# Turning the tiles of v: VectorE blocks of 32x32 and transfers of 128-byte rows in place of TensorE

## The chip, the cores and the metric

The kernel runs on one core of a Trainium2 chip. The metric is the device time of one execution in microseconds (us). Before the change it is 1673.76 us, the median of three runs (1672.92 to 1674.23).

## What is computed

A backbone of two layers over 256 latent tokens and 256 context tokens of width 1024. Layer 0 mixes tokens with a convolution module, layer 1 with a bidirectional mLSTM of four heads; an MLP follows each. The change lies in layer 1, in the features of the mLSTM:

```python
up = u @ w_up
xm, z = up[..., :MLSTM_INNER], up[..., MLSTM_INNER:]      # MLSTM_INNER = 2048
xc = jax.nn.silu(dwconv(xm, w_conv) + b_conv)
q, k, v = xc @ w_q, xc @ w_k, xm @ w_v
gates = jnp.concatenate([q, k, v], axis=-1) @ w_gate + b_gate
...
num = jnp.einsum('bhts,bhsd->bhtd', scores, vc) + ...     # v with tokens as the contraction
```

All data is float32. The scan needs v with the tokens on the partitions; the product xm @ w_v is made with the features on the partitions, so each tile of v has to be turned.

## The kernel before

Each weight tile is loaded by SyncE's queue (`raw_load`, L143, 1 MB into one of three buffers `raw`), cut into two halves of 128x1024, and each half is split into a high part `wh` (a cast on ScalarE, L149) and a low part `wl` (a subtraction on VectorE, L150). Four buffers of each exist. A half then feeds 24 matmuls (L180, L183, L184: high by high, high by low, low by high, for eight blocks of the contraction). A scheduler of the framework sets the order of each engine's instructions; the program's order is its priority. Every transfer is given one of eight completion semaphores in turn (DMAHW0 to DMAHW7), over all queues, and waits until the transfer that had the semaphore before it has landed.

The stage that matters here makes v: `gemm_steps(wv, range(8), xm, T, v_epi)`. It yields sixteen tiles, m = 0 to 15, of 128 features by 512 tokens (four blocks of 128 tokens). `v_epi` (L1220) copies a tile out of PSUM to `vt` on ScalarE. Turning it is deferred: `v_out(m, vt)` is put in the list `late`, and `flush()` empties the list when the next even m is done, so two tiles are turned at a time. `v_out` first adds the tile's share of the gates for every fourth m (L1211, four matmuls), then turns the tile and writes it to a DRAM buffer `v_dr[head]` of shape 128 tokens x 4 blocks x 512 features, from which the attention part loads it later. The turned tile passes through one of the four buffers of the tag E.

Beside this stage the same loop loads `wqT` (two loads of 1 MB per two halves in its first part), multiplies it by the gate weights (L772, sixteen small matmuls at a time), and in its second part streams `ada_w` through VectorE (L417 loads, L421 and L425) and prepares the tiles `u` and `xc` of the queries (`xc_load`, L149 and L150 on 128x256). After it come the queries (L195, L196), whose weights `wq` go through `raw`, `wh` and `wl` as well.

Of the kernel before, what the change touches and what calls it, by code (L numbers as in the profile page):

```python
# [14 lines left out]
P = 128  # L15
# [55 lines left out]
def hybrid_kernel(ctx: ExitStack, tc: tile.TileContext, xT, vecs_d, wdw_d, ada0_w, ada_w, wg_d, pw1a, pw1, pw2, w1_0, w2_0,  # L71
                  w1_1, w2_1, up_x, up_z, wv, wo, bo_d, wk, wq, wqT, wdown, rows_d, out):
    nc = tc.nc
# [10 lines left out]
    def nm(s):  # L84
        uid[0] += 1
        return f"{s}_{uid[0]}"
# [3 lines left out]
    def tmp(tag, dt=F32):  # L90
        return tp.tile([P, T], dt, tag=tag, name=nm(tag), bufs={"E": 4, "S": 2, "L": 2, "F": 1}[tag])
# [8 lines left out]
    def psum(tag="mm"):  # L100
        return pp.tile([P, 512], F32, tag=tag, name=nm(tag), bufs={"mm": 3, "ln": 2, "fl": 1, "cv": 2}[tag])
# [23 lines left out]
    ident = con.tile([P, P], F32, name="ident")  # L125
# [1024 lines left out]
    v_dr = [dp.tile([P, 4, DH], F32, name=f"v_dr{h}") for h in range(H)]  # L1150
# [18 lines left out]
    for f in range(0, DT, 2):  # L1169
        t, tr = tmp("S"), psum("cv")  # L1170
# [39 lines left out]
    def gate_acc(j, w, t, last=False):  # L1210
        nc.tensor.matmul(gps[32 * j:32 * j + 32, :], w, t, start=j not in seen, stop=last,  # L1211
                         tile_position=(0, 32 * j), skip_group_check=True)
        seen.add(j)
# [4 lines left out]
    def v_epi(m, ps):  # L1218
        vt = B("vt").rearrange("p a b -> p (a b)")[:, :T]
        nc.scalar.copy(vt, ps)  # L1220
        vts.append(vt)
        if m % 2 == 0:
            flush()
        late.append(lambda: v_out(m, vt))

    def v_out(m, vt):
        if m % 4 == 3:
            for j in range(4):
                gate_acc(j, wgv[:, m - 3 + j, :], vts[m - 3 + j])
        tr = psum("ln")  # L1230
        for b in range(4):
            nc.tensor.transpose(tr[:, b * P:(b + 1) * P], vt[:, b * P:(b + 1) * P], ident)
        vk = tmp("E")
        nc.scalar.copy(vk, tr)
        nc.scalar.dma_start(v_dr[m // 4][:, :, (m % 4) * P:(m % 4 + 1) * P], vk.rearrange("p (b c) -> p b c", b=4))

    late = []

# [752 lines left out]
```

## Time and profile before

| | |
|---|---|
| median of 3 runs | 1673.76 us (1672.92 to 1674.23) |
| the profiled execution | 1674.57 us, span 1672.9 us, mean TensorE clock 0.998 |
| TensorE (PE) busy | 1660.0 us |
| VectorE (DVE), ScalarE (ACT) busy | 1034.3 and 744.0 us |
| DMA | 301.63 MB, 180 GB/s over the span |
| turns of v on TensorE (L1232) | 64 of 128x128, first at 765.0, last at 927.1 us |
| copies of the turned tiles (L1234) | 16 on ScalarE, 594 ns each |
| transfers to v_dr (L1235) | 16 of 256 KB, issued by ScalarE's queue |

How to read it: a line names the source line, the engine, the operation, the output and inputs, and the shape; behind the bar stand busy time, the mean duration of one, and the idle time before it with what ended it. Timeline rows have the start in us from the span's start and the duration. PEld is TensorE's weight load, which overlaps the matmuls; ACTq and SPq are the DMA issues of ScalarE and SyncE; q1 is SyncE's DMA queue and q10 ScalarE's, with packets, MB and the share of 16 engines that the packets took.

### The profile page before, as it was taken

How to read it: one execution, taken by the hardware profiler on the slowest of the kernel's cores; microseconds unless marked ns; L12 is line 12 of the kernel's file. 1: busy time of each engine (PE TensorE's matmuls, PEld its weight loads, DVE VectorE, ACT ScalarE, POOL GpSimd, SP SyncE). 2: the span in 40 equal slices, each digit the busy share in tenths (PEclk: the TensorE clock that was granted, in tenths of full speed). 3: DMA queues.
4: the chain of work that ended last, by engine and by line, in shares of the span. 5: the costliest groups of instructions: out<-in, count | busy, mean ns of one | idle time of the engine just before them, and what ended most of it. 6: DMA issues, size and time to landing. Idle time of an engine off the chain costs nothing. (4 is left out here: it accounts for less than half of the span.)

```text
span 1672.9 us, 22919 instructions
## 1 busy us (share of the span) xinstructions
PE 1660.0 (99%) x8928; PEld 1366.8 (82%) x8928; DVE 1034.3 (62%) x1877; ACT 744.0 (44%) x1196; POOL 14.3 (1%) x64
## 2 busy tenths in 40 slices
PE   9999999999999999999999999999999999999998
PEld 6665898888888998877788899888878888778887
DVE  6555895666635776752143653564389876786677
ACT  4313573232324476652232532442368654555453
POOL 0000000000000000000000000000000000000001
PEclk9999999999999999999999999999999999999999
DMA  9565213444424065556685753455375555675452
GB/s 356 202 215 207 88 71 114 151 135 139 142 101 151 1 210 187 183 195 248 254 271 168 262 175 120 136 205 170 133 246 192 193 210 211 249 272 190 182 186 92
DMA packets 73902, 301.63 MB, mean 180 GB/s; under 512 B 7519, under 2 KB 23683, under 8 KB 43969
## 3 DMA queue, kind: packets, MB, share of 16 engines
q1 hardware_dynamic: 56080, 285.44, 48.5%
q10 hardware_dynamic: 17712, 14.72, 2.6%
q8 instruction: 70, 1.15, 0.3%
q14 instruction: 40, 0.32, 0.1%
HBM read 284.37 MB, written 15.77 MB: 179 GB/s over the span
## 5 line engine op out<-in xcount | busy, mean ns | idle before, releaser
L150 DVE TENSOR_TENSOR wl<-raw,wh 128x1024 fp32r<-128x1024 f32 x344 | 418.7, 1221 | 275.7 <-ACT wh L149 273.2
L149 ACT CAST wh<-raw 128x1024 fp32r<-128x1024 f32 x344 | 359.3, 1052 | 509.6 <-PE mm L183 277.2
L183 PE MATMUL mm<-u,wh 128*128 128x512 f32 (+1 forms) x808 | 291.7, 361 | 0.2 <-DVE u L610 0.2
L180 PE MATMUL mm<-u,wh 128*128 128x512 f32 (+1 forms) x680 | 244.4, 360 | 0.1
L184 PE MATMUL mm<-u,wl 128*128 128x512 f32 (+1 forms) x680 | 241.4, 356 | 0.0
L183 PEld LDWEIGHTS mm<-u,wh 128*128 128x128 f32 x808 | 152.6, 189 | 23.1 <-issue 1.0
L180 PEld LDWEIGHTS mm<-u,wh 128*128 128x128 f32 x680 | 128.5, 189 | 25.7 <-issue 6.4
L184 PEld LDWEIGHTS mm<-u,wl 128*128 128x128 f32 x680 | 128.4, 189 | 18.8 <-issue 1.0
L211 PE MATMUL mm<-wh,xl 128*128 128x512 f32 x256 | 101.1, 395 | 0.0
L180 PE MATMUL mm<-xm,wh 128*128 128x512 f32 x256 | 101.0, 395 | 0.0
L212 PE MATMUL mm<-wh,xl 128*128 128x512 f32 x256 | 100.1, 391 | 0.0
L184 PE MATMUL mm<-xm,wl 128*128 128x512 f32 x256 | 99.7, 390 | 0.0
L213 PE MATMUL mm<-wl,xl 128*128 128x512 f32 x256 | 99.2, 391 | 0.1
L180 PE MATMUL mm<-hid,wh 128*128 128x512 f32 (+1 forms) x256 | 93.3, 364 | 0.0
L183 PE MATMUL mm<-hid,wh 128*128 128x512 f32 (+1 forms) x256 | 92.9, 363 | 0.0
L184 PE MATMUL mm<-hid,wl 128*128 128x512 f32 (+1 forms) x256 | 92.8, 363 | 0.0
L195 PE MATMUL mm<-x,wh 128*128 128x512 f32 x232 | 81.1, 398 | 0.0
L425 DVE SCALAR_TENSOR_TENSOR S<-ar,cs,S 128x512 f32<-128x512 f32 x56 | 40.8, 749 | 59.0 <-DMA ar<-ada_w 58.9
L183 PE MATMUL mm<-qq,wh 128*128 128x272 f32 x256 | 73.9, 289 | 0.0
L180 PE MATMUL mm<-qq,wh 128*128 128x272 f32 x256 | 73.5, 288 | 0.0
L184 PE MATMUL mm<-qq,wl 128*128 128x272 f32 x256 | 73.5, 288 | 0.0
L195 PE MATMUL mm<-u,wh 128*128 128x512 f32 x192 | 68.7, 399 | 0.0
(535 smaller groups left out, 3265.5 us busy)
## 6 DMA issues: line engine op xcount, KB each, us to landing
raw<-w SPq DMA_DIRECT2D x64, 1024.0 KB, 4.8
raw<-wo SPq DMA_DIRECT2D x32, 1024.0 KB, 4.8
raw<-ada_w SPq DMA_DIRECT2D x22, 1024.0 KB, 6.7
ar<-ada_w SPq DMA_DIRECT2D x80, 256.0 KB, 3.7
raw<-wv SPq DMA_DIRECT2D x16, 1024.0 KB, 7.1
raw<-wqT SPq DMA_DIRECT2D x16, 1024.0 KB, 6.2
raw<-wq SPq DMA_DIRECT2D x16, 1024.0 KB, 4.9
raw<-wk SPq DMA_DIRECT2D x16, 1024.0 KB, 4.9
```

The source lines that it names most:

```text
L149: c = nc.scalar.copy(hi, src)
L150: lastsub[0] = nc.vector.tensor_tensor(lo, src, hi.bitcast(F32), op=ALU.subtract).ins
L180: a = nc.tensor.matmul(ps, wh, xh, start=start, stop=False)
L183: nc.tensor.matmul(ps, wh, xl, start=False, stop=False)
L184: lastmm[0] = nc.tensor.matmul(ps, wl, xh, start=False, stop=stop).ins
L195: todo = [lambda s_, e_: nc.tensor.matmul(ps, wh, r[0], start=s_, stop=e_), lambda s_, e_: nc.tensor.matmul(ps[:, :n], wl, r[0][:, :n], st ...
L211: nc.tensor.matmul(ps, xh, wh, start=start, stop=False)
L212: nc.tensor.matmul(ps, xl, wh, start=False, stop=False)
L213: nc.tensor.matmul(ps, xh, wl, start=False, stop=stop)
L425: nc.vector.scalar_tensor_tensor(a, w, c, a, op0=ALU.mult, op1=ALU.add)
```

## The change

For every tile the four turns on TensorE and the copy out of PSUM are replaced by one VectorE instruction that turns the tile in blocks of 32x32 in place. What the blocks leave undone, bringing each block to its place, is left to the transfer: one of 128x4 rows of 512 bytes becomes four, one for each 32 partitions, and each writes 32x16 rows of 128 bytes (64 KB).

```diff
         if m % 4 == 3:
             for j in range(4):
                 gate_acc(j, wgv[:, m - 3 + j, :], vts[m - 3 + j])
-        tr = psum("ln")
-        for b in range(4):
-            nc.tensor.transpose(tr[:, b * P:(b + 1) * P], vt[:, b * P:(b + 1) * P], ident)
         vk = tmp("E")
-        nc.scalar.copy(vk, tr)
-        nc.scalar.dma_start(v_dr[m // 4][:, :, (m % 4) * P:(m % 4 + 1) * P], vk.rearrange("p (b c) -> p b c", b=4))
+        nc.vector.transpose(vk, vt)
+        for q in range(4):
+            f0 = (m % 4) * P + 32 * q
+            nc.scalar.dma_start(v_dr[m // 4][:, :, f0:f0 + 32].rearrange("(q i) b j -> i b q j", i=32),
+                                vk[32 * q:32 * q + 32, :].rearrange("i (b q j) -> i b q j", b=4, q=4))
```

The scheduler places the instructions anew. First, TensorE before, where tiles 0 and 1 are turned: mm_6870 is the sum of tile m=2, mm_6871 of m=3, mm_7032 of m=4, and wh_7002 and wh_7036 are the high parts of two weight halves.

```order
L184 MATMUL mm_6870<-xm_6713,wl_6945 128x512
L1232 MATMUL ln_6974<-ident,vt_6825 128x128 x4
L1232 MATMUL ln_6982<-ident,vt_6868 128x128 x4
L772 MATMUL fl_6827<-raw_6990,wgq_578 32x512 x4
L772 MATMUL fl_6827<-raw_6996,wgq_578 32x512 x4
L180 MATMUL mm_6871<-xm_6358,wh_7002 128x512
...
L184 MATMUL mm_6871<-xm_6713,wl_7003 128x512
L180 MATMUL mm_7032<-xm_5950,wh_7036 128x512
```

After the change the two rows of L1232 are gone from here and nothing else moves; the half behind L772 uses weights that were split earlier, and the one after that uses wh_7036 (wh_7032 in the changed kernel). ScalarE before, at the cast of those weights, with the semaphores that each row waits for:

```order
L149 CAST wh_7036<-raw_7034 128x1024 [waits DMAHW7_49,PE_49]
L1220 COPY vt_6972<-mm_6870 128x512 [waits PE_49]
L1234 COPY E_6979<-ln_6974 128x512 [waits DMAHW2_49,PE_49]
L1234 COPY E_6987<-ln_6982 128x512 [waits PE_49]
L1235 DMA v_dr_5286<-E_6979 512x1x128 [waits Activation_49]
L1235 DMA v_dr_5286<-E_6987 512x1x128 [waits Activation_49]
L149 CAST wh_7076<-raw_7034 128x1024
```

And after, at the same place, where E_6974 and E_6980 are the turned tiles 0 and 1 and DVE_49 is VectorE's semaphore:

```order
L1234 DMA v_dr_5286<-E_6974 128x4x32 [waits DVE_49]
L1234 DMA v_dr_5286<-E_6974 128x4x32 x2
L1234 DMA v_dr_5286<-E_6974 128x4x32 [waits DMAHW3_49]
L1234 DMA v_dr_5286<-E_6980 128x4x32 [waits DMAHW4_49,DVE_49]
L1234 DMA v_dr_5286<-E_6980 128x4x32 [waits DMAHW5_49]
L1234 DMA v_dr_5286<-E_6980 128x4x32 [waits DMAHW6_49]
L1220 COPY vt_6972<-mm_6870 128x512 [waits PE_49]
L1234 DMA v_dr_5286<-E_6980 128x4x32 [waits DMAHW0_49]
L149 CAST wh_7032<-raw_7030 128x1024 [waits DMAHW2_49]
L149 CAST wh_7072<-raw_7030 128x1024
```

Eight issues now stand ahead of the cast, and five of them wait for an earlier transfer (DMAHW6 and DMAHW0 there are the first two transfers of tile 0). At the end of the stage, ScalarE before, around the copy of tile 15 (vt_8037); wh_8181 and wh_8209 are the wq weights of the second half of the contraction:

```order
L149 CAST wh_8181<-raw_8179 128x1024 [waits DMAHW6_49,DVE_49]
L149 CAST u_8096<-raw_8076 128x256 [waits PE_49]
L149 CAST u_8097<-raw_8076 128x256 [waits PE_49]
L149 CAST wh_8209<-raw_8179 128x1024 [waits DVE_49,PE_49]
L1220 COPY vt_8037<-mm_7893 128x512 [waits PE_49]
L1234 COPY E_8047<-ln_8042 128x512 [waits PE_49]
L1235 DMA v_dr_5289<-E_8047 512x1x128 [waits DMAHW2_49,Activation_49]
```

After, from the copy of tile 15 (vt_8009) on; between the last two rows stand eight casts of xc; wh_8149 holds the same weights as wh_8181 before:

```order
L1220 COPY vt_8009<-mm_7869 128x512 [waits PE_49]
L1234 DMA v_dr_5289<-E_8014 128x4x32 [waits DMAHW6_49]
L1234 DMA v_dr_5289<-E_8024 128x4x32 [waits DMAHW0_49,DVE_49]
L1234 DMA v_dr_5289<-E_8024 128x4x32 [waits DMAHW1_49]
L1234 DMA v_dr_5289<-E_8024 128x4x32 [waits DMAHW2_49]
L1234 DMA v_dr_5289<-E_8024 128x4x32 [waits DMAHW3_49]
L149 CAST u_8059<-raw_8044 128x256
L149 CAST u_8064<-raw_8044 128x256
L149 CAST u_8065<-raw_8044 128x256
...
L149 CAST wh_8149<-raw_8147 128x1024
```

The cast of these weights has moved from ahead of tile 15 to behind its transfers and the casts of u and xc.

## The prediction

> **What bounds the kernel now.** I read the page first: engines, then the chain that ended last.
>
> ```profile
> span 1672.9 us, 22919 instructions
> PE 1660.0 (99%) x8928; PEld 1366.8 (82%) x8928; DVE 1034.3 (62%) x1877; ACT 744.0 (44%) x1196; POOL 14.3 (1%) x64
> PE 12%; DVE 0%; DVEq 0%; issue 0%
> ```
>
> TensorE is busy for 1660.0 of 1672.9 us and the chain that could be followed is TensorE alone. So TensorE work that goes away shortens the run, unless something else then comes late. The stage to look at is the one that makes v, about 740 to 930 us; the busy table of that stretch and its groups by shape:
>
> ```profile
> core 0: us, PE busy (x) PEld busy (x) DVE busy (x) ACT busy (x) POOL busy (x), PEclk, DMA share, GB/s
> 800.00:850.00 50.00, 50.00 (x255) 36.69 (x254) 14.51 (x21) 16.14 (x26) 0.00 (x0) 1.00 0.74 270
> sum 195.00, PE 195.00 PEld 147.30 DVE 66.52 ACT 64.00 POOL 0.00; mean PE 39.00 PEld 29.46 DVE 13.30 ACT 12.80 POOL 0.00
> ```
>
> ```profile
> L150 DVE TENSOR_TENSOR wl<-raw,wh 128x1024 fp32r<-128x1024 f32 x32 | 38.6, 1221 | 68.4 <-ACT wh L149 68.3
> L425 DVE SCALAR_TENSOR_TENSOR S<-ar,cs,S 128x512 f32<-128x512 f32 x14 | 10.5, 751 | 36.0 <-DMA ar<-ada_w 36.0
> L1232 PE MATMUL ln<-ident,vt 128*128 128x128 f32 x64 | 9.2, 276 | 0.0
> L1234 ACT COPY E<-ln 128x512 f32<-128x512 f32 x16 | 8.9, 594 | 1.6 <-PE ln L1232 1.6
> L421 DVE TENSOR_SCALAR S<-ar,cs 128x512 f32<-128x512 f32 x2 | 1.0, 482 | 2.9 <-DMA ar<-ada_w 2.9
> ```
>
> TensorE is full at full clock, VectorE and ScalarE work a third of the time, and the DMA engines are the next thing that is nearly used up (0.74 of the stretch from 800).
>
> **What goes away.** 64 turns on TensorE and 16 copies on ScalarE. The 276 ns of a turn is a pipelined duration; what it holds TensorE for is read from starts (TensorE's timeline):
>
> ```profile
> 764.76 0.39 PE L184 MATMUL mm<-xm,wl 128*128 128x512 f32 x1
> 764.99 1.03 PE L1232 MATMUL ln<-ident,vt 128*128 128x128 f32 x8
> 765.95 1.92 PE L772 MATMUL fl<-raw,wgq 128*32 128x512 f32 x16
> 767.81 0.50 PE L180 MATMUL mm<-xm,wh 128*128 128x512 f32 x1
> 773.17 0.39 PE L184 MATMUL mm<-xm,wl 128*128 128x512 f32 x1
> 773.40 0.39 PE L180 MATMUL mm<-xm,wh 128*128 128x512 f32 x1
> 778.61 0.39 PE L184 MATMUL mm<-xm,wl 128*128 128x512 f32 x1
> 778.93 1.92 PE L772 MATMUL fl<-raw,wgq 128*32 128x512 f32 x16
> ```
>
> From L184 to L772 it takes 1.19 us with eight turns between (764.76 to 765.95) and 0.32 without (778.61 to 778.93): eight turns cost 0.87 us, 0.11 each, and 64 cost 7.0 us. That is the whole possible gain, 0.42% of the run. It is the first term: -7.0.
>
> **What is added, off the path.** Sixteen block turns on VectorE. No row shows one; a pass over 128x512 takes 482 ns (L421) to 751 ns (L425), and an added instruction gains nothing; 0.6 us, 10 us in all, against 66.5 us of VectorE work in 195. Each waits for its vt, and VectorE's splits wl stand behind it. The buffer it writes is one of four, so it also waits for the transfers of four tiles earlier, some 40 us back.
>
> The transfers: 16 of 128x4 rows of 512 bytes become 64 of 512 rows of 128 bytes. The issues on ScalarE's queue (two source lines), and queue counts in three stretches (768 to 780, 560 to 620, 760 to 935):
>
> ```profile
> L1235 ACTq DMA_DIRECT2D v_dr<-E x16: 520/521/1534, 768.8 to 928.0; - x16
> DMA to landing us min/median/max: 2.4/4.1/10.5
> ```
>
> ```profile
> q10 hardware_dynamic: 1056, 0.52, 14.6%
> ```
>
> ```profile
> q10 hardware_dynamic: 1440, 1.31, 6.3%
> ```
>
> ```profile
> q1 hardware_dynamic: 6883, 36.60, 59.6%
> q10 hardware_dynamic: 8525, 4.29, 8.2%
> ```
>
> An issue takes 0.521 us; the new ones make 512 rows as well, so I take the same, up to 0.8 back to back (1.534 was the longest). ScalarE then spends 4 x 0.521 = 2.08 us a tile instead of 0.594 + 0.521 = 1.12: 15 us more in 195, room enough, if nothing urgent stands behind. Time on the DMA engines: 14.6% of 12 us x 16 engines is 28.0 us for 1056 packets, 26.5 ns at a mean of 496 bytes; 6.3% of 60 x 16 is 60.5 us for 1440, 42.0 ns at 910. The line through both gives 12.7 ns at 128 bytes (my estimate); the bounds are 12.7 and 26.5, and I take the low end because both rows lie on a slope with length. 32,768 rows are 2048 an engine: 26 us (54 at 26.5 ns) instead of 13.6. Loads use 104 us of the 175 per engine (59.6%), so the engines stay below full either way. A flush of two tiles holds them 256 x 12.7 ns = 3.3 us instead of 1.7, so a load that runs beside it lands up to 1.6 us later, within the cover of 4 us shown below.
>
> [...]
>
> **What comes late instead.** Each transfer carries one of eight semaphores in turn and waits until the last transfer on it has landed; ScalarE waits in order, and the casts of the weights wh stand behind. Two places matter.
>
> First, the flush of tiles 0 and 1, whose transfers stand ahead of the cast of the next weights. ScalarE's timeline there:
>
> ```profile
> 757.04 0.34 ACTq L1204 DMA_DIRECT2D zs_dr<-E  x1
> 766.75 1.05 ACT L149 CAST wh<-raw 128x1024 fp32r<-128x1024 f32 x1 [9.75 <-DMA raw<-wv]
> ```
>
> By the order, the cast at 766.75 serves the half that starts at 773.40. With the turns gone that half starts at 772.5 and wants wl 0.45 us in, so the cast may start until 770.6. Ahead of it now the last transfer of tile 1 waits for the second of tile 0, issued about 757.9 (behind zs_dr at 757.04, 0.34, and one issue of 0.52). It must land by 770.0: 12 us, where 10.5 was the longest. So nothing is lost if the rows keep to that; 1 us for every us beyond. The later flushes have the same cover of 4 to 5 us. For all of them I put 0.9 us, between 0 and 4.
>
> Second, the end of the stage. Tile 15 is ready when m=15 ends, and ScalarE has then five issues, three u casts and eight xc casts ahead of the cast of the wq weights which TensorE wants next; before, these weights were cast ahead of tile 15. Rows of TensorE, then of ScalarE:
>
> ```profile
> 923.54 0.39 PE L184 MATMUL mm<-xm,wl 128*128 128x512 f32 x1
> 923.77 0.60 PE L1232 MATMUL ln<-ident,vt 128*128 128x128 f32 x4
> 932.52 0.39 PE L195 MATMUL mm<-u,wh 128*128 128x512 f32 x1
> 932.75 0.28 PE L196 MATMUL mm<-u,wl 128*128 128x256 f32 x1
> ```
>
> ```profile
> 919.99 0.75 ACT L149 CAST u<-raw 128x256 fp32r<-128x256 f32 x2 [0.79 <-ACT E L1234]
> 924.69 0.58 ACT L1220 COPY vt<-mm 128x512 f32<-128x512 f32 x1
> 928.57 2.26 ACT L149 CAST xc<-raw 128x256 fp32r<-128x256 f32 x7 [0.28 <-ACT xc L149]
> ```
>
> Count from 923.77, the end of m=15 on TensorE. It wanted the weights of the second contraction half at 932.52, 8.75 us on; without its two groups of four turns (0.9) that is 7.85, and wl 0.23 later, 8.1. ScalarE: vt from 0.16 (its last matmul ends 923.93) to 0.75; last issue of tile 14 to 1.27; block turn of tile 15 to about 1.4; four issues to 3.5; three u casts at 0.375 to 4.6; eight xc casts at 0.32 to 7.2; cast 1.05 to 8.25; wl on VectorE 1.22 to 9.5. TensorE waits 9.5 - 8.1 = 1.4 us; with issues at 0.8 us, 2.8. I take 2.1.
>
> **The sum.** -7.0 + 2.1 + 0.9 = -4.0 us. The profiled execution took 1674.57 us (span 1672.9 and 1.67 around it, untouched): 1670.57. It lies 0.81 above the median of 1673.76, so the prediction is **1669.8 us**.
>
> **The rivals.**
> - All hidden: no wait takes the turns' place, for instance because TensorE's order reaches wl later. For it: VectorE and ScalarE are idle two thirds of the stage. Against: the end of the stage above. 1673.76 - 7.0 = 1666.8.
> - The gain is eaten: issues near 1 us each, or waits of 4 us in the flushes, as a stage that lives on loads (0.74 busy) gives back what TensorE saves. -7.0 + 2.8 + 3 = -1.2: 1672.6.
> - Slower through ScalarE's queue: the 128-byte rows share the engines with 1 MB loads, so a transfer lands after 15 us instead of 12 and each of eight flushes holds the next cast 3 us too long: -7 + 24, 1691. It decides from a landing of about 13 us on. For it: 10.5 has been seen with a quarter of the transfers. Against: the new transfers carry 64 KB instead of 256.
> [...]
> - The change doesn't do what it says: excluded, the built order has 64 fewer turns.
>
> **How the numbers follow.** Forecast 0.34, all hidden 0.10, eaten 0.16, ScalarE's queue 0.24, short rows 0.16. The two slower cases together get 0.40 because the price of a short row, on which both hang, is an extrapolation beyond the last row shown. Within 0.2% (3.3 us, about what a measurement of this kernel can tell from no change) is the eaten case alone: faster 0.44, same 0.16, slower 0.40. The forecast's own range is 1667 to 1670.4. The range that holds 8 in 10 starts at 1666.8, takes in the ScalarE case to 1692 and leaves out the short rows (0.16).
>
> **What would show it.** Right: no L1232 on TensorE; about 0.32 us from L184 to L772 at each flush; one wait of 1.5 to 3 us on wh or wl at the first query matmuls; v_dr issues near 0.52 us. Wrong: a q10 share in the stage above 25%, L149 behind L1234 with waits on v_dr transfers, repeated TensorE waits between 765 and 920, or block turns over 1.2 us.

## The result, and the profile after

The changed kernel took 1683.78 us (1682.70 to 1687.12) against 1673.99 before: ratio 1.0059, interval 1.0048 to 1.0071. It is slower by 9.8 us, where 4 us less were forecast. The parts of the page that answer to those of before (the head, the engines, the chain that ended last):

```profile
span 1681.1 us, 22846 instructions
PE 1658.7 (99%) x8864; PEld 1362.5 (81%) x8864; DVE 1044.1 (62%) x1893; ACT 733.0 (44%) x1180; POOL 14.3 (1%) x64
PE 89%; DMA 5%; DVE 4%; ACT 1%; issue 1%; DVEq 0%; ACTq 0%; SPq 0%
```

The 64 turns are gone from TensorE (8864 instructions for 8928), but the chain, which could be followed only along TensorE before, now leads through DMA and VectorE. The waits of TensorE between 740 and 1000 us, in total, times and longest (before there is no such row):

```profile
PE mm L184 <- DVE wl L150: 4.5, 1, 4.5
PE mm L195 <- DVE E L206: 2.9, 2, 1.8
PE mm L196 <- DVE wl L150: 1.3, 1, 1.3
PE mm L195 <- ACT wh L149: 1.2, 2, 0.6
```

Where the time went is read from the starts of the same matmuls. First TensorE's timeline, two rows of L180 on either side of the long wait, before and after the change:

```profile
890.21 0.39 PE L180 MATMUL mm<-xm,wh 128*128 128x512 f32 x1
903.15 0.39 PE L180 MATMUL mm<-xm,wh 128*128 128x512 f32 x1
```

```profile
885.79 0.39 PE L180 MATMUL mm<-xm,wh 128*128 128x512 f32 x1
905.45 0.39 PE L180 MATMUL mm<-xm,wh 128*128 128x512 f32 x1
```

Then the query matmuls of L195 in the view of their line (durations, first and last start), before and after:

```profile
L195 PE MATMUL mm<-u,wh x192: 387/397/502, 925.3 to 1109.1; 128*128 128x512 f32 x192
```

```profile
L195 PE MATMUL mm<-u,wh x192: 387/396/505, 926.2 to 1116.4; 128*128 128x512 f32 x192
```

At the first row of L180 the change had brought 4.42 us (890.21 to 885.79), as the forty turns up to there promised. At the second, sixteen L180 later, it was 2.30 us behind (903.15 to 905.45): 6.7 us were lost in between. That is net: the eight turns of tiles 10 and 11, which lie in this stretch before the change, are 0.9 us of gain, so 7.6 us were lost. The queries began 0.9 us late and ended 7.3 us late: 6.4 us more. The last 0.9 us up to the end of the span (8.2) come later; TensorE waits there for 1.7 us at L1402, and this was not followed.

**The first loss** is one wait and the slow clock behind it. The timeline of the changed kernel, rows of VectorE, then of ScalarE, then one of TensorE (start, duration, operation, and in brackets the idle time before it):

```profile
880.49 0.75 DVE L425 SCALAR_TENSOR_TENSOR S<-ar,cs,S 128x512 f32<-128x512 f32 x1 [3.84 <-DMA ar<-ada_w]
881.16 0.70 DVE L1231 STREAM_TRANSPOSE E<-vt 128x512 f32<-128x512 f32 x1
885.71 0.75 DVE L425 SCALAR_TENSOR_TENSOR S<-ar,cs,S 128x512 f32<-128x512 f32 x1 [3.85 <-DMA ar<-ada_w]
889.65 0.75 DVE L425 SCALAR_TENSOR_TENSOR S<-ar,cs,S 128x512 f32<-128x512 f32 x1 [3.19 <-DMA ar<-ada_w]
893.57 0.75 DVE L425 SCALAR_TENSOR_TENSOR S<-ar,cs,S 128x512 f32<-128x512 f32 x1 [3.17 <-DMA ar<-ada_w]
894.24 3.49 DVE L150 TENSOR_TENSOR wl<-raw,wh 128x1024 fp32r<-128x1024 f32 x3
877.26 0.82 ACTq L1234 DMA_DIRECT2D v_dr<-E  x1
881.89 0.58 ACTq L1234 DMA_DIRECT2D v_dr<-E  x1
885.68 2.95 ACT L149 CAST wh<-raw 128x1024 fp32r<-128x1024 f32 x3 [7.86 <-DMA v_dr<-E]
895.51 0.80 PE L184 MATMUL mm<-xm,wl 128*128 128x512 f32 x1 [4.50 <-DVE wl L150]
```

TensorE's busy time and granted clock there (the table of stretches; the clock is the column behind POOL):

```profile
890.00:895.00 5.00, 1.02 (x6) 0.30 (x2) 1.83 (x3) 0.84 (x2) 0.00 (x0) 0.96 0.18 52
895.00:900.00 5.00, 4.49 (x11) 3.52 (x12) 4.85 (x6) 0.00 (x0) 0.00 (x0) 0.50 0.80 271
900.00:905.00 5.00, 5.00 (x21) 4.06 (x20) 1.14 (x2) 0.59 (x1) 0.00 (x0) 0.85 0.92 262
```

Read it in order of time. VectorE's sum of ada_w at 880.49 waited 3.84 us for its load. The turn of tile 11 stood behind it, at 881.16. ScalarE's next transfer, the first of that tile, could go only when the turn was done, at 881.89; ScalarE's queue had been free since 878.08 (877.26 and 0.82). The cast of the next weights stood behind the four transfers of the tile, until 885.68; the third of these also waited 1.2 us, and by the numbers in the kernel's order the semaphore that it waited for (DMAHW0) had last been used by a transfer of tile 10, not by a load. The split wl of these weights then stood on VectorE behind three more sums of ada_w, whose loads come one at a time, some 4 us apart. It began at 894.24, and TensorE, which wanted it at 891.01, went on at 895.51. The rows of VectorE's order say the same; before, at most two sums stood between two splits:

```
L1231 STREAM_TRANSPOSE E_7826<-vt_7686 128x512
L425 SCALAR_TENSOR_TENSOR S_7723<-ar_7832,cs,S_7723 128x512
L425 SCALAR_TENSOR_TENSOR S_7723<-ar_7865,cs,S_7723 128x512
L425 SCALAR_TENSOR_TENSOR S_7723<-ar_7900,cs,S_7723 128x512
L150 TENSOR_TENSOR wl_7836<-raw_7784,wh_7835 128x1024
```

After the wait the clock was granted at 0.50 and then 0.85. In stretches of 1 us it is 1.00 up to 894, 0.82 from 894 to 895, still in the wait, 0.50 from 895 to 901, 0.77 from 901 to 902 and 1.00 from there. So TensorE, at work again from 895.51, ran some 6 us at 0.50 (up to about 901.5), its matmuls 0.43 us apart (twelve from 896.11 to 901.23) and 0.23 afterwards, and by that lost 3.0 us (an estimate, half of the 6). With the 4.50 us of the wait that makes 7.5 of the 7.6.

**The second loss** begins at the third load of wq. SyncE's timeline of the changed kernel, then a row of ScalarE and one of VectorE:

```profile
917.15 0.33 SPq L143 DMA_DIRECT2D raw<-wq  x1
928.16 0.33 SPq L1274 DMA_DIRECT2D rk<-wg_d  x1
930.95 0.33 SPq L143 DMA_DIRECT2D raw<-wq  x1
929.39 1.02 ACT L149 CAST u<-raw 128x256 fp32r<-128x256 f32 x3 [3.44 <-DMA v_dr<-E]
929.83 1.10 DVE L150 TENSOR_TENSOR u<-raw,u 128x256 fp32r<-128x256 f32 x3 [3.13 <-ACT u L149]
```

And before, the row of SyncE with two loads of wq (at 914.30 and, 9.97 us being the time to the end of the second, near 924), and the last split of u on VectorE:

```profile
914.30 9.97 SPq L143 DMA_DIRECT2D raw<-wq  x2
923.50 0.42 DVE L150 TENSOR_TENSOR u<-raw,u 128x256 fp32r<-128x256 f32 x1 [0.20 <-ACT u L149]
```

There are three buffers `raw`. The third load of wq takes the one from which the tiles u are split, so it must wait for the last of these splits. In both kernels it goes 0.02 us after that split has ended: at 923.94 before (923.92) and at 930.95 after (930.93). The last three splits come late because their casts stand on ScalarE behind the transfers of tile 15, which wait for the turn of that tile. The small load rk now stands ahead of this load of wq, but it has gone at 928.16, well before the buffer comes free. The loads of wq stay late through the queries, where TensorE waits five times.

### The profile page after: what moved, and what is told of

Same layout as the page of the kernel before. It is cut to its first block, busy times and chain, and to the rows that moved or that the text cites. A ratio compares the mean times of both kernels' runs of the same rounds, so it can differ in the third digit from the quotient of the medians.

```text
span 1681.1 us, 22846 instructions
## 1 busy us (share of the span) xinstructions
PE 1658.7 (99%) x8864; PEld 1362.5 (81%) x8864; DVE 1044.1 (62%) x1893; ACT 733.0 (44%) x1180; POOL 14.3 (1%) x64
## 4 chain that ended last, share of the span: by engine, by line
PE 89%; DMA 5%; DVE 4%; ACT 1%; issue 1%; DVEq 0%; ACTq 0%; SPq 0%
PE mm L180 16%; PE mm L184 16%; PE mm L183 16%; PE mm L195 5%; DMA ar<-ada_w 4%; PE mm L211 4%; PE mm L213 4%; PE mm L212 4%; PE mm L196 3%; PE cv L211 2%; PE cv L212 2%; PE cv L213 2%; PE fl L342 1%; PE ln L180 1%; DVE wl L150 1%; PE cv L855 1%
## 5 line engine op out<-in xcount | busy, mean ns | idle before, releaser
L180 PE MATMUL mm<-u,wh 128*128 128x512 f32 (+1 forms) x680 | 244.4, 360 | 0.0
L184 PE MATMUL mm<-u,wl 128*128 128x512 f32 (+1 forms) x680 | 241.5, 356 | 0.0
L180 PEld LDWEIGHTS mm<-u,wh 128*128 128x128 f32 x680 | 128.5, 189 | 25.6 <-issue 5.9
L184 PEld LDWEIGHTS mm<-u,wl 128*128 128x128 f32 x680 | 128.4, 189 | 18.9 <-issue 1.0
L184 PE MATMUL mm<-xm,wl 128*128 128x512 f32 x256 | 101.2, 395 | 4.5 <-DVE wl L150 4.5
L180 PE MATMUL mm<-xm,wh 128*128 128x512 f32 x256 | 102.0, 398 | 0.0
L180 PE MATMUL mm<-hid,wh 128*128 128x512 f32 (+1 forms) x256 | 93.3, 364 | 0.0
L184 PE MATMUL mm<-hid,wl 128*128 128x512 f32 (+1 forms) x256 | 92.8, 363 | 0.0
L195 PE MATMUL mm<-x,wh 128*128 128x512 f32 x232 | 81.1, 398 | 0.0
L180 PE MATMUL mm<-qq,wh 128*128 128x272 f32 x256 | 73.5, 289 | 0.0
L184 PE MATMUL mm<-qq,wl 128*128 128x272 f32 x256 | 73.5, 288 | 0.0
L195 PE MATMUL mm<-u,wh 128*128 128x512 f32 x192 | 69.3, 400 | 4.1 <-DVE E L206 2.9
```

The source lines that it names most:

```text
L180: a = nc.tensor.matmul(ps, wh, xh, start=start, stop=False)
L184: lastmm[0] = nc.tensor.matmul(ps, wl, xh, start=False, stop=stop).ins
L195: todo = [lambda s_, e_: nc.tensor.matmul(ps, wh, r[0], start=s_, stop=e_), lambda s_, e_: nc.tensor.matmul(ps[:, :n], wl, r[0][:, :n], st ...
```

## The experiments

The theory: the loss comes from ScalarE's queue, from the semaphores that its 64 transfers share with SyncE's loads, and from the order that this gives on VectorE and SyncE. The rivals: the 128-byte rows load the DMA engines; VectorE's turns stand in the way.

**The transfers on another queue.** `nc.scalar.dma_start(v_dr...)` in `v_out` becomes `nc.gpsimd.dma_start`.

> The changed kernel with its 64 transfers issued by GpSimd's queue instead of ScalarE's; rows, sizes and VectorE's turns are the same. GpSimd's transfers have eight semaphores of their own. Theory A (the loss comes from ScalarE's queue, whose issues wait for semaphores that SyncE's loads of ada_w and of the weights hold, and from the order that this gives): no TensorE wait is left at 891 us, and the gain of the turns remains: 1667 to 1670 us. Theory B (128-byte rows slow the DMA engines and so the loads): the rows are still there, 1681 to 1686. Theory C (VectorE's turns stand in the way of the splits): also 1681 to 1686.

1669.48 us (1667.24 to 1674.22), ratio 0.9974 (0.9963 to 0.9985). Its span is 1665.5 us, and no row of TensorE's waits is left between 740 and 1000 us. In its order the transfers carry semaphores of their own (DMASW0 to DMASW7). GpSimd issues them, and its waits for the turns (143.8 us in all) hold TensorE up nowhere in this stage (the view of v_dr; then the queue count of 765 to 920 us):

```profile
L1234 POOL DMA_DIRECT2D v_dr<-E x64: 739/739/944, 757.4 to 922.6; - x64
  DVE E L1231: 143.8, 14
```

```profile
q0 software_dynamic: 1836, 3.74, 8.7%
```

The turns on VectorE are the same, and the gain is there, so the third theory falls. The second is not settled by this run: the transfers ask for the same short rows, but GpSimd's queue counts 1836 packets for them, of 2 KB on average. This version leaves nothing out, and it beats both kernels.

**Rows and number taken apart.** One transfer a tile, with rows of 128 bytes at other places of v_dr, and one with the rows of before.

```diff
-        for q in range(4): ... (four transfers)
+        nc.scalar.dma_start(v_dr[m // 4].rearrange("p b (q r j) -> p (b q) r j", q=4, r=4)[:, :, m % 4, :],
+                            vk.rearrange("p (x j) -> p x j", j=32))
```

> VectorE's turns kept; one transfer a tile on ScalarE's queue, of 2048 rows of 128 bytes, whose pieces go to other places of v_dr (the bringing of each block to its place is left out). 16 transfers as before the change, the same 32,768 short rows. Theory A (number of transfers and whose semaphore they wait for): 1667 to 1671. Theory B (short rows): 1681 to 1686, and TensorE waits again between 885 and 970 us.

> VectorE's turns kept; the transfer of before, one of 512 rows of 512 bytes a tile (the bringing of each block to its place is left out). Neither short rows nor more transfers. Theories A and B: 1667 to 1670, and its distance to the kernel with 16 transfers of short rows is the price of the rows: under 1 us by A, over 10 by B. Theory C (VectorE's turns): 1681 or more.

1667.53 us (1666.64 to 1668.15; 0.9959, 0.9947 to 0.9972) and 1667.82 (1666.91 to 1671.09; 0.9967, 0.9955 to 0.9980). The short rows cost no time here. What they cost the DMA engines, from the queue counts of 757 to 925 us, first of the kernel with short rows, then of that with long ones:

```profile
q10 hardware_dynamic: 32068, 4.43, 16.2%
```

```profile
q10 hardware_dynamic: 8727, 4.57, 9.1%
```

16.2% of 168 us x 16 engines is 435 us for 32,068 packets, 13.6 ns each; the long rows take 28.0. So neither short rows nor VectorE's turns made the loss: the second theory falls too.

**Two transfers a tile.** As the first of these, cut in two halves of 1024 rows.

> As the kernel with one transfer of 2048 short rows a tile (the bringing of each block to its place is left out), but two transfers of 1024 rows: 32 in all, between 16 (1667.5) and 64 (1683.8). If the loss grows with each transfer: 1671 to 1676. If it begins only where the transfers of a flush (8 with 64, 4 with 32) outnumber the semaphores that are free: 1667 to 1669.

1669.55 us (1667.92 to 1670.68; 0.9974, 0.9964 to 0.9984), in the gap between the two expectations: 2 us for sixteen more transfers, and 14 for the 32 after these. So the loss does not grow evenly. The 2 us themselves are hardly clear of the noise, as the intervals of the two ratios overlap (0.9947 to 0.9972 and 0.9964 to 0.9984).

**More transfers, nothing else.** The kernel before, with its turns on TensorE:

```diff
-        nc.scalar.dma_start(v_dr[m // 4][:, :, (m % 4) * P:(m % 4 + 1) * P], vk.rearrange("p (b c) -> p b c", b=4))
+        for b in range(4):
+            nc.scalar.dma_start(v_dr[m // 4][:, b, (m % 4) * P:(m % 4 + 1) * P], vk[:, b * P:(b + 1) * P])
```

> The kernel before, with its turns on TensorE and its copies on ScalarE, but each tile's transfer cut into four of 128 rows of 512 bytes (64 transfers, long rows). Theory A (number of transfers on ScalarE's queue): slower than before by about what the held order still lost, 1676 to 1682. Theories of the rows or of VectorE's turns: 1673.5 to 1675.

1679.32 us (1678.32 to 1682.30; 1.0030, 1.0020 to 1.0041), within what was expected. Long rows and no turn on VectorE, and still 5 us slower. The place of the first loss is another one, a copy of the gates (L777) on ScalarE, and again the first query weights (TensorE's waits):

```profile
PE fl L780 <- ACT F L777: 3.1, 1, 3.1
PE mm L195 <- ACT wh L149: 1.9, 2, 0.9
```

So 64 transfers on ScalarE's queue cost time without short rows and without turns on VectorE. Which of its waits cost what was not taken apart.

**Which tiles.** VectorE's turns for tiles 0 to 7 only, and for 8 to 15 only (`if m < 8:` and `if m >= 8:` around the new code).

> VectorE's turns and the short rows for tiles 0 to 7 only, most of whose transfers are issued before the loads of ada_w begin at 836 us; tiles 8 to 15 as before. Theory A with the semaphores held by ada_w: half of the turns' 7.0 us is gained and nothing lost, 1669.5 to 1671.5. If issues on ScalarE cost wherever they are: 1672 to 1677.

> VectorE's turns and the 128-byte rows for tiles 8 to 15 only, tiles 0 to 7 as before: the counterpart to the kernel with tiles 0 to 7 (1669.7). If the whole loss of the changed kernel arises where the ada_w loads run (from 836 us), it is all here, and 3.5 us of gain less: 1685 to 1688. If it arises in all flushes alike: 1676 to 1681.

1669.68 us (1669.36 to 1671.14; 0.9975, 0.9966 to 0.9984) and 1683.60 (1682.70 to 1691.07; 1.0069, 1.0056 to 1.0083). The first eight tiles gain 4.4 us, a little more than the 3.5 that their turns are worth, and TensorE waits for nothing in the stage. The last eight alone lose 13 us (against the 1670.4 that half the turns would give), of the 16.3 that the whole change loses against the kernel with sixteen transfers; the remaining 3 us were not followed. So four transfers a tile on ScalarE's queue did no harm in the first eight tiles; they did in the last eight, where the loads of ada_w and the end of the stage meet them.

The two also bear on the shared semaphores. SyncE's loads do wait for transfers of v_dr, which they never did before, in the changed kernel and then in the one with tiles 0 to 7 (SyncE's waits from 740 to 960 us: total, times, longest):

```profile
SPq L143 <- DMA v_dr<-E: 20.3, 5, 8.0
```

```profile
SPq L143 <- DMA v_dr<-E: 23.2, 5, 9.5
```

The second kernel has as much of this and loses nothing. That the shared semaphores have a part in the loss is therefore not shown.

**VectorE's order held.** In the stage of v the sums of ada_w are kept in the program's order.

```diff
-                    nc.vector.scalar_tensor_tensor(a, w, c, a, op0=ALU.mult, op1=ALU.add)
+                    o = nc.vector.scalar_tensor_tensor(a, w, c, a, op0=ALU.mult, op1=ALU.add)
+                    if vpin[0]:
+                        tc.keep_in_program_order(o)
```

> The changed kernel with VectorE's sums of ada_w held in the program's order during the stage of v, so that they no longer stand three in a row ahead of a split wl; ScalarE's order and the 64 transfers stay. If VectorE's order alone makes the loss: 1668 to 1672. If ScalarE's waits for the semaphores alone make it: 1682 to 1685 as in the changed kernel. I expect both to count: the wait of 4.5 us at 891 and the slow clock behind it (2.2 us more) go, the late loads of wq stay: 1676 to 1679.

1674.84 us (1671.09 to 1678.23; 1.0003, 0.9994 to 1.0012): 9 us of the loss are gone, a little more than expected. ScalarE waits as before for the same flush (8.05 us), but the split is no longer behind the sums (its timeline, a row of ScalarE and one of VectorE):

```profile
886.44 2.96 ACT L149 CAST wh<-raw 128x1024 fp32r<-128x1024 f32 x3 [8.05 <-DMA v_dr<-E]
887.53 1.23 DVE L150 TENSOR_TENSOR wl<-raw,wh 128x1024 fp32r<-128x1024 f32 x1 [0.52 <-ACT wh L149]
```

So the wait of ScalarE alone was covered; the order of VectorE behind it was not.

**The last flush as before.** Tiles 14 and 15 turned by TensorE with one transfer each (`if m < 14:` around the new code), in the changed kernel and in the one with VectorE's order held.

> The changed kernel with only the last flush (tiles 14 and 15, at the end of the stage) as before the change: turned by TensorE, one transfer each. In SyncE's order the third load of wq then stands ahead of the small load rk again. If the waits of TensorE in the queries come from that flush, 5 to 6 us of them go and 0.9 us of turns return: 1678 to 1680, and the wait of 4.5 us at about 891 us stays. If they are the lasting effect of the wait at 891: 1684 to 1685.

> The kernel with VectorE's sums held in order (1674.8) with the last flush as before the change. If the rest of its loss comes from that flush: 1668.5 to 1671, TensorE without waits after 920 us. If it comes from ScalarE's waits in the earlier flushes: 1674 to 1676.

1677.88 us (1677.09 to 1681.90; 1.0023, 1.0012 to 1.0034) and 1670.21 (1668.14 to 1672.84; 0.9974, 0.9964 to 0.9984). The first takes 5.9 us off the changed kernel and keeps the wait at 895 us (4.4 us there). The last split of u ends at 926.26 there, and the third load of wq goes at 926.28, ahead of rk, instead of at 930.95. With both edits TensorE waits once between 740 and 1000 us, for 0.6 us. From the timeline of the first, SyncE's row, and from TensorE's waits of the second the only one:

```profile
916.86 9.75 SPq L143 DMA_DIRECT2D raw<-wq  x2
```

```profile
PE mm L185 <- DVE wl L150: 0.6, 1, 0.6
```

The two edits together bring 13.6 of the 16.3 us that lie between the changed kernel and the one with sixteen transfers; the two tiles on TensorE are 0.9 of the rest, and 1.8 stay open.

**Without the loads of ada_w.** In the stage of v the sums read one block that is loaded once.

> The changed kernel, in which the sums of ada_w in the stage of v read one block that is loaded once, so that fifteen of its sixteen loads there are left out; VectorE's sums, the 64 transfers and the short rows stay. If ScalarE waits for semaphores that these loads hold, and VectorE for the loads themselves: 1667 to 1671. If it is the number of issues on ScalarE, whatever else is loaded: 1676 or more.

> The comparison to it: the kernel before with the same fifteen loads left out. TensorE hardly waits in the kernel before, so 1673 to 1675 by every theory.

1674.24 us (1670.82 to 1677.01; 1.0004, 0.9995 to 1.0013) against 1674.09 (1673.04 to 1675.11). It lies between the two expectations: without the loads 9.5 us of the loss are gone, and the long wait with them, but not the rest. That is what the held order gave. The last flush, which this leaves alone, is the likely remainder: ScalarE again waits 3.4 us for transfers of v_dr ahead of a cast of u, and the third load of wq again goes behind rk (rk at 920.68, wq at 923.19). It was not taken away here.

**The loads of ada_w on GpSimd.** L417 becomes `nc.gpsimd.dma_start`, in the kernel with VectorE's order held and in the kernel before. This moves all 80 loads of the kernel, not only those of the stage of v.

> The kernel with VectorE's sums held in order, and besides the loads of ada_w issued by GpSimd's queue, so that they no longer hold any of the eight semaphores that ScalarE's 64 transfers wait for; the transfers stay on ScalarE's queue with all their issues. If the loss that was left there (1674.8 against 1667.5) is ScalarE waiting for semaphores that the ada_w loads hold: 1667 to 1670.5. If it is the number of issues on ScalarE itself, or semaphores in general: 1673 to 1676.

> The comparison to it: the kernel before, with the loads of ada_w issued by GpSimd's queue. Every theory: 1673 to 1675, as the kernel before. Should it be faster by itself by over 2 us, the other run's gain is not that of the semaphores alone.

1689.65 us (1.0091, 1.0078 to 1.0105) and 1701.07 (1.0161, 1.0147 to 1.0175). The comparison failed its own expectation by 27 us, so this pair says nothing on the semaphores that the ada_w loads hold. Why these loads are so dear on that queue was not followed.

## Why the prediction failed

- **The turns' gain (7.0) was right**: 4.4 us up to 886 us, and 0.32 us from L184 to L772 (777.73 to 778.05). With sixteen transfers, which is all of the change but the number and form of the transfers, 6.5 us are measured.
- **The short rows were right**: 12.7 ns estimated, 12.5 in the changed kernel and 13.6 with one transfer a tile (the first from the row below, the queue count of the changed kernel from 765 to 920 us: 14.6% of 155 x 16 us for 28,905 packets). The chance of 0.16 on slow short rows rested on a price of a row that no run shows. By the byte a short row was dearer (13.6 ns for 128 bytes, 28.0 for 512), but the run was no longer for it (1667.53 us with the short rows, 1667.82 with the long ones).

```profile
q10 hardware_dynamic: 28905, 3.59, 14.6%
```

- **VectorE's turns were right in effect** (0.706 us each, 0.6 assumed; the group's row below, of 740 to 960 us). That its splits stand behind the turns was said; that the sums of ada_w stand ahead of a turn, and so ahead of ScalarE's transfers and casts, was not.

```profile
L1231 DVE STREAM_TRANSPOSE E<-vt 128x512 f32<-128x512 f32 x16 | 11.2, 706 | 37.1 <-ACT vt L1220 30.9 <-DMA raw<-wqT 6.2
```

- **The term of the flushes (+0.9, between 0 and 4) is the step that failed.** It followed the first flush, which indeed cost nothing, and took "the later flushes have the same cover" over to the rest. From 836 us on the loads of ada_w run, and the flush of tiles 10 and 11 cost 7.6 us by itself. The term counted ScalarE's wait, which its cover did hold (8.05 us without harm in the run with VectorE's order held). It left out VectorE's new order, in which a sum stands ahead of the turn and three more stand between the turn and the split. The issues were also 0.642 us in the median, not 0.521.
- **The term of the end of the stage (+2.1) was too small, and this is the second step that failed.** Where it looked it was near: 1.2 us of waits for wh at the first query matmuls. It also counted the three casts of u that stand behind the transfers. But it did not ask who waits for their splits: SyncE's third load of wq, which takes the buffer that they free and goes 7 us later. The queries lost 6.4 us in all, and 5.9 go when the last flush is as before.
- **The sum**, with what was measured: -7.0 for the turns, 7.6 in place of 0.9, 6.8 in place of 2.1 (the 6.4, and the 0.4 of turns that the queries' time had before), and 0.9 later that it did not have. That is 8.3, and the span grew by 8.2.
- **The rival by ScalarE's queue (1691) had the sign and the queue right, and the mechanism wrong.** It asked for landings of 13 us and waits in each of eight flushes. The longest landing was 10.8 us, and only flushes of the second half lost time: one by VectorE's order, one by the late casts of u. That it came nearer to the measured time than the forecast did is luck.

## What to carry to other kernels

When a change multiplies transfers on a queue, follow every queue that they meet, in the new order: who waits for the instruction that feeds them, what is queued behind it, and which loads on other queues wait for a buffer that comes free behind them. A cover found at the first of many flushes holds for that one; check the one where other streams run. Work that leaves the bounding engine can lose more than it gains if urgent work waits behind its transfers: here GpSimd's queue, behind which TensorE waited for nothing between 740 and 1000 us, turned a loss of 9.8 us into a gain of 4.5.

## What the runs showed that was not expected

A wait of 4.5 us on TensorE cost 7.6, with the clock at 0.50 for some 6 us behind it. And GpSimd's queue, which took the 64 transfers of short rows without loss (1669.5), made the kernel before 27 us slower when it got the loads of ada_w.
